# The last 128 tokens of the gate stage: from features on partitions to tokens on partitions

## The chip, the cores and the metric

The kernel runs on one core of one Trainium2 chip. A core has five engines with a queue each: TensorE (PE in the profile, with its weight loads as PEld), VectorE (DVE), ScalarE (ACT), GpSimd (POOL) and SyncE (SP, which here only issues transfers). Each queue is worked off in order; the queues wait for one another by semaphores. The metric is the time of one execution on the device, in microseconds (us).

## The reference

One encoder layer over 1024 tokens of 1024 features, in float32. Only its end matters here:

```python
hn = rmsnorm(h, norm_ple_g)
gate = jax.nn.sigmoid(hn @ w_ple_gate + b_ple_gate)   # (1024 x 1024) @ (1024 x 1024)
h = h + gate * (p @ w_ple)                            # p: 1024 x 256
return rmsnorm(h, final_g)                            # y = x * rsqrt(mean(x*x) + eps) * g
```

Before it come a pooling mixer and a chunked attention with their projections, and a gated MLP.

## The kernel before

All activations lie transposed in SBUF: features on the 128 partitions in eight tiles (`H[0]` to `H[7]`), tokens along the free axis. Every large product is done as three matmuls (`mm3`, L130 to L132) on operands that are split into a high and a low part (`hi`, `lo`), in a reduced-precision float32 format; the three add up in one PSUM bank. Moving operands are at most 512 columns wide.

The gate stage (from `ple_mm` on) is the last one. It runs over 18 items `(d, a, b)`: feature tile `d` of the output, tokens `a` to `b`. For the first token half there are eight items of 512 tokens. For the second half there are six items of 512 tokens, and for the last two feature tiles four items of 256 tokens. An item is

- `gate_mm`: 8 x 3 matmuls with the gate weights as stationary operand and the normed activations (`hp[0]` or `hp[1]`) as moving operand, into bank 2, 3 or 7;
- `ple_mm`: 2 x 3 matmuls for the per-layer embedding, into bank 5 or 6;
- `gate_out`: sigmoid on ACT (L1150), times the embedding product on DVE (L1151), added to `H` on DVE (L1152);
- `Norm.add`: square on ACT (L647), added up over feature tiles on DVE (L649);
- a scaling of the item by the final norm's gain on ACT (L1205).

With features on partitions, the sum of squares of a token runs over partitions and over feature tiles. So the final norm of a stretch of tokens (a `Norm` object in `lasts`) ends in four more steps: `sums`, one small matmul against a column of ones for each 128 tokens (L655, L657) with a VectorE step (L658) and a power of -1/2 on POOL (L659); `rows`, which spreads the result over all partitions by PE transposes (L663); and `emit`, which multiplies `H` by it on DVE (L1169) in pieces of 1024 elements per partition and issues a 512 KB store for each piece (L1170), by turns on the SP and the ACT queue. The second half has two such norms, for tokens 512 to 767 and 768 to 1023. The first of these is emitted in the middle of the last item; the second stands alone at the end of the kernel.

PE's order is the order of the code. Of the other engines a scheduler sets the order, except where `keep_in_program_order` pins it.

Of the kernel before, what the change touches and what calls it, by code (L numbers as in the profile page):

```python
# [6 lines left out]
F32 = mybir.dt.float32  # L7
F32R = mybir.dt.float32r
AF = mybir.ActivationFunctionType
ALU = mybir.AluOpType  # L10

P = 128
SEQ = 1024
D = 1024
KT = D // P
# [7 lines left out]
MAX_REL = 128  # L23
WINDOWS = (2, 4, 8, 16)
HIST = 16
EPS = 1e-6
BIG = 3.0e38

# [53 lines left out]


def trunk(tc, xT, pT, vecs, w_qk0, w_in, w_v, bias, counts, pool_w, w_out, w_up, w_down,
          w_gate, w_ple, out):
    nc = tc.nc
    act, dve, pe, pool, sp = nc.scalar, nc.vector, nc.tensor, nc.gpsimd, nc.sync

    with tc.tile_pool(name="sb", bufs=1) as sb, \
# [6 lines left out]
        def region(z, dt):  # L96
            a, b = spans[z]
            return sb.tile([P, (b - a) * 256], dt, name=f"R{z}", tag=f"R{z}")

        Rs = [region(z, F32R) for z in range(5)]  # L100
        F = sb.tile([P, 15616], F32, name="F")
        ident = sb.tile([P, P], F32, name="ident")
        vec = sb.tile([P, NVEC], F32, name="vec")
        small = sb.tile([P, 80], F32, name="small")
        PS = pp.tile([P, 8, 512], F32, name="PS")
# [16 lines left out]
        def f(kb, n):  # L122
            return F[:, int(kb * KW):int(kb * KW) + n]
# [15 lines left out]
        mhalf = small[:, 0:1]  # L139
# [27 lines left out]
        qk32 = [f(38 + 4 * s, 1024) for s in range(2)]  # L167
        U = f(38, 4 * (HIST + SEQ)).rearrange("p (g t) -> p g t", g=4)
        T1 = f(54.25, 272)
# [75 lines left out]
        for t in range(NTOK):  # L245
            pe.matmul(PS[:, 7, t:t + 1], xraw[0][:, t * P:(t + 1) * P], ones, start=True, stop=True)
        dve.tensor_scalar(rstd_tok, PS[:, 7, 0:NTOK], 1.0 / D, EPS, ALU.mult, ALU.add)
        pool.tensor_tensor(rstd_tok, rstd_tok, mhalf.to_broadcast([P, NTOK]), ALU.pow)
# [79 lines left out]
        def keys(i):  # L328
            t = i % NTOK
            k0 = max(0, t - 4)  # L330
            return i // NTOK, t, k0, t + 1 - k0
# [111 lines left out]
        def project_u(g):  # L443
            def evac(h, ps):
                hs = slice(h * 512, (h + 1) * 512)
                dve.tensor_tensor(U[:, g, HIST + h * 512:HIST + (h + 1) * 512], ps, rstd_bc[:, hs], ALU.mult)
            pool.memset(U[:, g, 0:HIST], 0.0)
            yield from project(g, evac)
            win = WINDOWS[g]
            eng = pool if g >= 2 else dve  # L450
            for q in (3, 2, 1, 0):
                n = HIST + 256
                u = U[:, g, q * 256:q * 256 + n]
# [9 lines left out]
        def pool_out(g, q, u, src, eng):  # L463

            win, n, f0 = WINDOWS[g], HIST + 256, HIST
            if q == 0:
                f0 = HIST + win
                eng.tensor_tensor(src[:, HIST:f0], src[:, HIST:f0], cnt[:, 0:win], ALU.mult)
# [103 lines left out]
        for i in range(NI + 3):  # L572
            if i >= 7:
                sums_due(i, (i - 6) // 2)
            if i < NI:
                h, t, k0, nk = keys(i)
# [43 lines left out]
        H = [f(8 + 4 * d, 1024) for d in range(KT)]  # L620
# [6 lines left out]
        class Norm:  # L627
# [24 lines left out]
            def sums(self):  # L652
                for t in range(self.nt):
                    ts_ = slice(t * P, (t + 1) * P)
                    pe.matmul(self.ssq[:, t:t + 1], self.acc[:, ts_], ones, start=True, stop=self.whole)  # L655
                    if not self.whole:
                        pe.matmul(self.ssq[:, t:t + 1], self.q[:, ts_], ones, start=False, stop=True)  # L657
                dve.tensor_scalar(self.s, self.ssq, 1.0 / D, EPS, ALU.mult, ALU.add)  # L658
                pool.tensor_tensor(self.s, self.s, mhalf.to_broadcast([P, self.nt]), ALU.pow)  # L659
# [149 lines left out]
        for z, d in enumerate((0, 4, 1, 5, 2, 6, 3, 7)):  # L809
            k = z // 2  # L810
# [218 lines left out]
        wg = [None] * KT  # L1029
        hp = [None, None]  # L1030
# [90 lines left out]
        pt = [(r(8 * k, 1024), r(8 * k + 4, 1024)) for k in range(2)]  # L1121
        wp = [(r(16 + 8 * k, 1024), r(20 + 8 * k, 1024)) for k in range(2)]
# [11 lines left out]
        def gate_mm(d, a, b, bank, middle=None):  # L1134
            ds_ = slice(d * P, (d + 1) * P)
            ts_ = slice(a % 512, a % 512 + b - a)
            for k in range(KT):
                hi, lo = hp[a // 512][k]
                mm3(PS[:, bank, 0:b - a], wg[k][:, ds_], wg[k][:, 1024:2048][:, ds_], hi[:, ts_], lo[:, ts_],
                    k == 0, k == KT - 1)  # L1140
                if k == 3 and middle:
                    middle()
# [21 lines left out]
        def emit(norm):  # L1164

            n = 1024 // (norm.nt * P)
            for z, d in enumerate(range(0, KT, n)):
                h_ = HH[:, d:d + n, norm.ts]
                dve.tensor_tensor(h_, h_, norm.out.unsqueeze(1).to_broadcast([P, n, norm.nt * P]), ALU.mult)  # L1169
                (sp, act)[z % 2].dma_start(  # L1170
                    out[d * P:(d + n) * P, norm.ts].rearrange("(e p) t -> p e t", p=P), h_)

        zt = [f(2 * s, 512) for s in range(4)]
        acc, sq = f(52.25, 512), f(54.25, 512)
        lasts = {(0, 512): Norm(slice(0, 512), f(40, 512), [f(42, 512)], 4, 1),
                 (512, 1024): Norm(slice(512, 1024), acc, [sq], 4, 1)}
        for z, ab in enumerate(((512, 768), (768, 1024))):
            zs = slice(256 * z, 256 * z + 256)
            lasts[ab] = Norm(slice(*ab), acc[:, zs], [sq[:, zs]], 4, z, z == 0)
            lasts[ab].n = 6  # L1180
        ple_banks, gate_banks = (5, 6), (2, 3, 7)
        items = ([(d, 0, 512) for d in range(KT)] + [(d, 512, 1024) for d in range(6)]
                 + [(d, a, a + 256) for a in (512, 768) for d in (6, 7)])

        def ended(ab):
            lasts[ab].rows()
            emit(lasts[ab])

        for i, (d, a, b) in enumerate(items):
            gate_mm(d, a, b, gate_banks[i % 3], (lambda: ended((512, 768))) if i == 17 else None)  # L1190
            if i == 0:
                continue
            if i == 16:
                lasts[512, 768].sums()
            if i == 1:
                norm_b.sums()
            if i == 2:
                norm_b.rows(rst2[:, HS[1]])
            for z in ((0, 1) if i == 1 else (i,)):
                dz, az, bz = items[z]  # L1200
                ple_mm(dz, az, bz, ple_banks[z % 2])
                gate_out(dz, az, bz, gate_banks[z % 3], ple_banks[z % 2], zt[z % 4])
                lasts[az, bz].add(dz)
                hz = H[dz][:, az:bz]
                act.activation(hz, hz, AF.Copy, scale=vec[:, C_GL + dz:C_GL + dz + 1])  # L1205
            if 3 <= i <= 6:
                normed2(2 * i - 6)
                normed2(2 * i - 5)
            if i == 8:
                lasts[0, 512].sums()  # L1210
            if i == 9:
                ended((0, 512))
        lasts[768, 1024].sums()
        ended((768, 1024))
        b_pool.__exit__(None, None, None)


def _layout(i):

    c = np.ascontiguousarray  # L1220
    x = i["x"][0]
    w_in = i["w_in"][0]
    w_up = i["w_up"][0]
    d = {}
    d["xT"] = c(x.T).reshape(KT, P, SEQ)
    d["pT"] = c(i["p"][0, 0].T).reshape(2, P, SEQ)

    def cols(v, n):
        return np.asarray(v).reshape(n, P).T

    cw = i["conv_w"][0]
    d["vecs"] = c(np.concatenate(
        [cols(i["norm_mix_g"][0], KT)] + [cols(cw[j], NF) for j in range(3)]
        + [cols(i["conv_b"][0], NF), cols(i["pool_b"][0], 4), cols(i["pool_scale"][0], 4)]
        + [cols(i[n], KT) for n in ("norm_ffn_g", "norm_ple_g", "b_ple_gate", "final_g")], axis=1))
    wt = w_in.reshape(KT, P, 16, P).transpose(2, 1, 0, 3)
    d["w_qk0"] = c(np.concatenate([wt[4], wt[8]], axis=2)).reshape(P, KT * 2 * P)
    d["w_in"] = c(wt[:12]).reshape(12, P, D)
    d["w_v"] = c(w_in[:, 1536:].reshape(KT, P, 2, 256).transpose(2, 1, 0, 3)).reshape(2, P, KT * 256)
    ii = np.arange(P)[:, None] + 512 - np.arange(BANDT * P)[None, :]  # L1240
    d["bias"] = c(i["rel_bias"][0][:, np.clip(ii, -MAX_REL, MAX_REL) + MAX_REL])
    d["counts"] = np.tile((1.0 / np.arange(1, 17)).astype(np.float32)[None, :], (P, 1))
    d["pool_w"] = c(i["pool_w"][0].transpose(1, 0, 2)).reshape(P, 512)
    d["w_out"] = c(i["w_out"][0].reshape(8, P, 2, 512).transpose(2, 0, 1, 3))
    d["w_up"] = c(w_up.reshape(KT, P, 2, NF, P).transpose(3, 2, 1, 0, 4)).reshape(NF, 2, P, D)
    d["w_down"] = c(i["w_down"][0].reshape(NF, P, D))
    d["w_gate"] = c(i["w_ple_gate"][0].reshape(KT, P, D))
    d["w_ple"] = c(i["w_ple"][0].reshape(2, P, D))
    return d


# [15 lines left out]
```

## Time and profile before

| | us |
|---|---|
| median of 3 runs | 1146.85 (1145.53 to 1147.0) |
| the profiled execution, its own time | 1144.99 |
| its span, first to last instruction | 1143.2 |
| busy PE / DVE / ACT / POOL in the span | 1124.7 / 886.8 / 580.4 / 282.3 |
| granted TensorE clock, mean | 0.996 |

The profiled execution is 1.86 us (0.16%) below the median of the other runs; 1.79 us of its time lie outside the span. Times below are us from the start of the span. In rows of the timeline the first number is the start, the second the duration; "x2" means two instructions that are drawn as one, from the first's start to the last's end. The matmul durations hold the pipeline's latency, so that two neighbours overlap: the pace is read from the starts.

### The profile page before, as it was taken

How to read it: one execution, taken by the hardware profiler on the slowest of the kernel's cores; microseconds unless marked ns; L12 is line 12 of the kernel's file. 1: busy time of each engine (PE TensorE's matmuls, PEld its weight loads, DVE VectorE, ACT ScalarE, POOL GpSimd, SP SyncE). 2: the span in 40 equal slices, each digit the busy share in tenths (PEclk: the TensorE clock that was granted, in tenths of full speed). 3: DMA queues.
4: the chain of work that ended last, by engine and by line, in shares of the span. 5: the costliest groups of instructions: out<-in, count | busy, mean ns of one | idle time of the engine just before them, and what ended most of it. 6: DMA issues, size and time to landing. Idle time of an engine off the chain costs nothing.

```text
span 1143.2 us, 15272 instructions
## 1 busy us (share of the span) xinstructions
PE 1124.7 (98%) x5517; PEld 944.7 (83%) x5517; DVE 886.8 (78%) x1371; ACT 580.4 (51%) x1001; POOL 282.3 (25%) x307
## 2 busy tenths in 40 slices
PE   9999999999999999999999999999999999999996
PEld 7988998888888877878888888888888888888886
DVE  7678878779656788888889888889797789757344
ACT  8568677765555543434443434344444567545222
POOL 0013334275002234645453434232000000000000
PEclk9999999999999999999999999999999999999998
DMA  7134756533500376554444321112683555310012
GB/s 265 38 86 114 164 118 178 121 85 130 184 19 10 137 213 175 137 138 123 149 118 112 91 100 39 65 38 78 222 281 109 167 185 169 115 48 1 1 74 75
DMA packets 62572, 133.46 MB, mean 117 GB/s; under 512 B 7392, under 2 KB 9696, under 8 KB 62048
## 3 DMA queue, kind: packets, MB, share of 16 engines
q1 hardware_dynamic: 49552, 100.96, 26.5%
q0 software_dynamic: 11200, 29.37, 12.8%
q10 hardware_dynamic: 1744, 2.17, 0.5%
q8 instruction: 43, 0.70, 0.3%
q14 instruction: 33, 0.27, 0.1%
HBM read 116.73 MB, written 45.09 MB: 142 GB/s over the span
## 4 chain that ended last, share of the span: by engine, by line
PE 83%; DVE 6%; ACT 3%; issue 3%; DMA 3%; POOL 1%; SPq 0%; DVEq 0%; POOLq 0%; ACTq 0%
PE PS L130 26%; PE PS L131 26%; PE PS L132 26%; PE PS L370 2%; ACT F L356 1%; PE PS L387 1%; PE PS L388 1%; DVE R L136 1%; DMA X<-in_w_up 1%; DVE B L378 1%; POOL SD L556 1%; DVE F L346 1%; DMA F<-in_xT 1%; DMA GD<-F 1%; POOL X L759 1%
## 5 line engine op out<-in xcount | busy, mean ns | idle before, releaser
L130 PE MATMUL PS<-R,R 128*128 128x512 f32 (+1 forms) x932 | 359.6, 386 | 0.6 <-ACT R L230 0.6
L132 PE MATMUL PS<-R,R 128*128 128x512 f32 (+1 forms) x932 | 355.8, 382 | 0.9 <-DVE R L136 0.9
L131 PE MATMUL PS<-R,R 128*128 128x512 f32 x868 | 338.0, 389 | 0.5 <-DVE R L231 0.5
L132 PEld LDWEIGHTS PS<-R,R 128*128 128x128 f32 x932 | 175.3, 188 | 35.6 <-DVE R L136 1.3
L130 PEld LDWEIGHTS PS<-R,R 128*128 128x128 f32 x932 | 175.3, 188 | 33.0 <-ACT R L230 1.0
L131 PEld LDWEIGHTS PS<-R,R 128*128 128x128 f32 x868 | 163.3, 188 | 32.7 <-DVE R L231 1.4
L131 PE MATMUL PS<-B 128*128 128x512 f32 x316 | 123.1, 390 | 0.4 <-DVE B L136 0.4
L130 PE MATMUL PS<-B 128*128 128x512 f32 x316 | 123.2, 390 | 0.0
L132 PE MATMUL PS<-B 128*128 128x512 f32 x316 | 123.1, 389 | 0.0
L759 POOL TENSOR_TENSOR X<-X 128x512 f32<-128x512 f32 x46 | 84.7, 1841 | 141.3 <-DMA X<-in_w_up 69.9
L135 ACT ACTIVATE R<-X 128x512 fp32r<-128x512 f32 x102 | 64.3, 632 | 103.5 <-PE PS L131 58.3
L135 ACT ACTIVATE R<-F 128x512 fp32r<-128x512 f32 (+1 forms) x116 | 69.2, 613 | 71.0 <-PE PS L131 35.7
L135 ACT ACTIVATE B<-F 128x512 fp32r<-128x512 f32 (+1 forms) x94 | 61.0, 649 | 82.8 <-PE PS L131 55.7
L136 DVE TENSOR_TENSOR R<-X,R 128x512 fp32r<-128x512 f32 x102 | 102.5, 1005 | 0.0
L136 DVE TENSOR_TENSOR R<-F,R 128x512 fp32r<-128x512 f32 (+1 forms) x112 | 85.7, 777 | 20.2 <-ACT R L135 19.6
L659 POOL TENSOR_TENSOR small<-small 128x4 f32<-128x4 f32 (+1 forms) x7 | 8.1, 1159 | 335.9 <-DVE small L658 335.9
L136 DVE TENSOR_TENSOR B<-F,B 128x512 fp32r<-128x512 f32 (+1 forms) x94 | 66.8, 714 | 29.1 <-ACT B L135 28.8
L131 PEld LDWEIGHTS PS<-B 128*128 128x128 f32 x316 | 59.3, 188 | 13.0 <-DVE B L136 0.8
L130 PEld LDWEIGHTS PS<-B 128*128 128x128 f32 x316 | 59.3, 188 | 12.4
L132 PEld LDWEIGHTS PS<-B 128*128 128x128 f32 x316 | 59.3, 188 | 12.4
L131 PE MATMUL PS<-B,R 128*128 128x256 f32 (+1 forms) x208 | 64.0, 308 | 0.0
L356 ACT ACTIVATE F<-F,small 128x640 f32<-128x640 f32 (+2 forms) x64 | 44.5, 696 | 24.3 <-DVE small L354 16.9
(171 smaller groups left out, 2081.8 us busy)
## 6 DMA issues: line engine op xcount, KB each, us to landing
SD<-in_w_down POOLq DMA_DIRECT2D x66, 256.0 KB, 4.9
X<-in_w_up SPq DMA_DIRECT2D x56, 256.0 KB, 3.0
F<-SD SPq DMA_DIRECT2D x49, 256.0 KB, 2.7
GD<-F SPq DMA_DIRECT2D x22, 512.0 KB, 2.6
R<-GD SPq DMA_DIRECT2D x44, 256.0 KB, 5.4
F<-in_w_down SPq DMA_DIRECT2D x33, 256.0 KB, 3.2
F<-in_w_up SPq DMA_DIRECT2D x29, 256.0 KB, 2.9
SD<-SD POOLq DMA_DIRECT2D x28, 256.0 KB, 3.1
```

The costliest lines, as they stand in the source:

```text
L130: pe.matmul(ps, ahi, bhi, start=first, stop=False, skip_group_check=more)
L131: pe.matmul(ps, ahi, blo, start=False, stop=False, skip_group_check=more)
L132: pe.matmul(ps, alo, bhi, start=False, stop=last, skip_group_check=more)
L135: act.activation(hi, src, AF.Copy)
L136: dve.tensor_tensor(lo, src, rv(hi), ALU.subtract)
L346: dve.tensor_tensor_reduce(S.rearrange("p (a b) -> p a b", a=2), PS[:, 4:6, 0:320], b.rearrange("p (a b) -> p a b", a=2), 1.0, BIG, ALU.ad ...
L356: act.activation(S[:, 0:n], S[:, 0:n], AF.Exp, bias=s_[:, 0:1], scale=-1.0, accum_out=s_[:, 1:2])
L370: pe.transpose(pst[:, j * P:(j + 1) * P], S[:, j * P:(j + 1) * P], ident)
L378: dve.tensor_tensor(lo, pst, rv(hi), ALU.subtract)
L387: pe.matmul(O, V[:, k, h], pt[:, 0, idx], start=n_ == 0, stop=False)
L388: pe.matmul(O, V[:, k, h], pt[:, 1, idx], start=False, stop=n_ == len(ks) - 1)
L759: pool.tensor_tensor(rawu[to], rawu[a], rawu[b], op)
```

## The change

The second token half is cut in two. Tokens 512 to 895 (`BODY` is 896) are computed as before, but as eight items of 384 tokens instead of six of 512 and four of 256, with one norm for all 384. The last 128 tokens (`TAIL`) are computed with tokens on partitions:

- eight PE transposes turn `H` of these tokens into `h_t` (banks 0 and 1);
- `ple_tail` and `gate_tail` swap the two operands of the products: the activations become the stationary operand, the weights the moving one, in slices of 512, 256 and 256 features;
- the arithmetic of a slice is a pinned sequence of six instructions: bias added (DVE), sigmoid (ACT), times the embedding product (DVE), plus `h_t` (DVE), square with a sum along the row (ACT, into `ss`), times the final gain (DVE);
- bias and gain now vary along the free axis, so a new input `rows` (128 x 2048, 1 MB, each row the same) is loaded on the SP queue into the region that held `hp[0]`;
- the norm's sum is along the row, so it needs no small matmuls and no transposes: two small DVE steps, one POOL power on 128x1, and then one scaling by that column, half of the features on ACT with a 256 KB store on the ACT queue, half on DVE with a 256 KB store on the SP queue;
- the norm of tokens 512 to 895 has its `sums` and `rows` between the matmuls of the first slice of the tail; its four stores all go by SP.

The output is one flat array, the first 896 tokens by features and the last 128 by tokens, put together outside of the timed part.

```diff
         def emit(norm):
             n = 1024 // (norm.nt * P)
+            dst = out[0:BODY * D].rearrange("(d t) -> d t", t=BODY)
             for z, d in enumerate(range(0, KT, n)):
                 h_ = HH[:, d:d + n, norm.ts]
                 dve.tensor_tensor(h_, h_, norm.out.unsqueeze(1).to_broadcast([P, n, norm.nt * P]), ALU.mult)
-                (sp, act)[z % 2].dma_start(
-                    out[d * P:(d + n) * P, norm.ts].rearrange("(e p) t -> p e t", p=P), h_)
+                (sp, act)[z % 2 if norm.ts.start == 0 else 0].dma_start(
+                    dst[d * P:(d + n) * P, norm.ts].rearrange("(e p) t -> p e t", p=P), h_)
...
-                 (512, 1024): Norm(slice(512, 1024), acc, [sq], 4, 1)}
-        for z, ab in enumerate(((512, 768), (768, 1024))):
...
+                 (512, BODY): Norm(slice(512, BODY), f(52.25, 512 - TAIL), [f(54.25, 512 - TAIL)], 4, 2)}
...
-        items = ([(d, 0, 512) for d in range(KT)] + [(d, 512, 1024) for d in range(6)]
-                 + [(d, a, a + 256) for a in (512, 768) for d in (6, 7)])
+        items = [(d, a, b) for a, b in ((0, 512), (512, BODY)) for d in range(KT)]
...
-            gate_mm(d, a, b, gate_banks[i % 3], (lambda: ended((512, 768))) if i == 17 else None)
+            gate_mm(d, a, b, gate_banks[i % 3])
...
-            if i == 16:
-                lasts[512, 768].sums()
...
-        lasts[768, 1024].sums()
-        ended((768, 1024))
+        Rs[2] = region(2, F32)
+        row_b, row_g, x_t, xg, o_t = [r(32 + 4 * k, D) for k in range(5)]
+        sp.dma_start(r(32, 2 * D), rows)
...
+        def ple_tail(z):
+            zs = slice(z * 512, (z + 1) * 512)
+            for k in range(2):
+                mm3(ple_t[:, zs], pt[k][0][:, BODY:SEQ], pt[k][1][:, BODY:SEQ], wp[k][0][:, zs], wp[k][1][:, zs],
+                    k == 0, k == 1)
+
+        def gate_tail(z, a, b, ps, hooks=()):
+            for k in range(KT):
+                hi, lo = [t[:, BODY - 512:512] for t in hp[1][k]]
+                mm3(ps, hi, lo, wg[k][:, a:b], wg[k][:, 1024 + a:1024 + b], k == 0, k == KT - 1)
+                if k in dict(hooks):
+                    dict(hooks)[k]()
+            t = x_t[:, a:b]
+            for ins in (lambda: dve.tensor_tensor(t, ps, row_b[:, a:b], ALU.add),
+                        lambda: act.activation(t, t, AF.Sigmoid),
+                        lambda: dve.tensor_tensor(t, ple_t[:, a:b], t, ALU.mult),
+                        lambda: dve.tensor_tensor(t, h_t[:, a:b], t, ALU.add),
+                        lambda: act.activation(o_t[:, a:b], t, AF.Square, accum_out=ss[:, z:z + 1]),
+                        lambda: dve.tensor_tensor(xg[:, a:b], t, row_g[:, a:b], ALU.mult)):
+                tc.keep_in_program_order(ins())
+
+        for d in range(KT):
+            pe.transpose(h_t[:, d * P:(d + 1) * P], H[d][:, BODY:SEQ], ident)
+        ple_tail(0)
+        gate_tail(0, 0, 512, PS[:, 3], ((3, lasts[512, BODY].sums), (6, lambda: ended((512, BODY)))))
+        ple_tail(1)
+        gate_tail(1, 512, 768, PS[:, 7, 0:256])
+        dve.tensor_scalar(ss[:, 3:4], ss[:, 0:1], ss[:, 1:2], D * EPS, ALU.add, ALU.add)
+        gate_tail(2, 768, 1024, PS[:, 7, 256:512])
+        s = ss[:, 4:5]
+        dve.tensor_scalar(s, ss[:, 2:3], ss[:, 3:4], 1.0 / D, ALU.add, ALU.mult)
+        pool.tensor_tensor(s, s, mhalf, ALU.pow)
+        dst = out[BODY * D:].rearrange("(t d) -> t d", d=D)
+        act.activation(o_t[:, 0:512], xg[:, 0:512], AF.Copy, scale=s)
+        act.dma_start(dst[:, 0:512], o_t[:, 0:512])
+        dve.tensor_scalar(o_t[:, 512:D], xg[:, 512:D], s, None, ALU.mult)
+        sp.dma_start(dst[:, 512:D], o_t[:, 512:D])
```

Lines of the changed kernel stand two or three further down than before (L660 is the old L658, L1172 the old L1169, L1173 the old L1170). Ahead of the second half's items no engine's order changes.

DVE's queue at the end of the program before, from the first sums step of the second half on: in a row of the queue stand the line, the operation, the output and the inputs (F is the SBUF buffer that holds `H`, PS is PSUM, small holds the norms' columns), and the shape.

```order
L658 TENSOR_SCALAR small<-PS 128x2
L1151 TENSOR_TENSOR F<-PS,F 128x256
L1152 TENSOR_TENSOR F<-F 128x256
L649 TENSOR_TENSOR F<-F 128x256
L1169 TENSOR_TENSOR F<-F,PS 128x4x256 x2
```

The two scalings of the first 256 tokens stand there ahead of the last item's L1151 and L1152; then come the last L658 and the last two scalings, L1169.

The same queue in the changed kernel, again from the sums step on (R_8392 is the region with the new rows and the tail's buffers):

```order
L660 TENSOR_SCALAR small<-PS 128x3
L1172 TENSOR_TENSOR F<-F,PS 128x2x384 x4
L1230 TENSOR_TENSOR R_8392<-PS,R_8392 128x512
L1232 TENSOR_TENSOR R_8392<-PS,R_8392 128x512
L1233 TENSOR_TENSOR R_8392<-PS,R_8392 128x512
L1235 TENSOR_TENSOR R_8392<-R_8392 128x512
L1230 TENSOR_TENSOR R_8392<-PS,R_8392 128x256
L1232 TENSOR_TENSOR R_8392<-PS,R_8392 128x256
L1233 TENSOR_TENSOR R_8392<-PS,R_8392 128x256
L1235 TENSOR_TENSOR R_8392<-R_8392 128x256
L1244 TENSOR_SCALAR small<-small 128x1
```

All four scalings of the body (L1172) have moved ahead of the whole arithmetic of the tail, and the three slices of the tail follow one another; the third slice's four instructions, L1247 and L1252 come last.

SP's queue at the end of the program before (its last loads are those of the embedding, then the stores):

```order
L929 DMA F<-in_w_down 128x512 x12
L929 DMA F<-in_pT 128x512 x2
L929 DMA F<-in_w_ple 128x512 x4
L1170 DMA out_h<-F 128x2x512 x2
L1170 DMA out_h<-F 128x4x256 x2
```

And in the changed kernel:

```order
L931 DMA F<-in_w_ple 128x512 x4
L931 DMA F<-in_pT 128x512 x2
L1212 DMA R_8392<-in_rows 128x2048
L1173 DMA out_h<-F 128x2x512 x2
L1173 DMA out_h<-F 128x2x384 x4
L1253 DMA out_h<-R_8392 128x512
```

The load of the new rows stands ahead of all stores, and the store of half of the tail behind the four of the body.

More of the change, by code (lines that the diff above doesn't have):

```diff
@@ L25 @@
 HIST = 16
+TAIL = 128
+BODY = SEQ - TAIL
 EPS = 1e-6
@@ L84, in trunk @@
 def trunk(tc, xT, pT, vecs, w_qk0, w_in, w_v, bias, counts, pool_w, w_out, w_up, w_down,
-          w_gate, w_ple, out):
+          w_gate, w_ple, rows, out):
     nc = tc.nc
@@ L1169, in emit @@
                 dve.tensor_tensor(h_, h_, norm.out.unsqueeze(1).to_broadcast([P, n, norm.nt * P]), ALU.mult)
-                (sp, act)[z % 2].dma_start(
-                    out[d * P:(d + n) * P, norm.ts].rearrange("(e p) t -> p e t", p=P), h_)
+                (sp, act)[z % 2 if norm.ts.start == 0 else 0].dma_start(
+                    dst[d * P:(d + n) * P, norm.ts].rearrange("(e p) t -> p e t", p=P), h_)
         zt = [f(2 * s, 512) for s in range(4)]
-        acc, sq = f(52.25, 512), f(54.25, 512)
         lasts = {(0, 512): Norm(slice(0, 512), f(40, 512), [f(42, 512)], 4, 1),
-                 (512, 1024): Norm(slice(512, 1024), acc, [sq], 4, 1)}
-        for z, ab in enumerate(((512, 768), (768, 1024))):
-            zs = slice(256 * z, 256 * z + 256)
-            lasts[ab] = Norm(slice(*ab), acc[:, zs], [sq[:, zs]], 4, z, z == 0)
-            lasts[ab].n = 6
+                 (512, BODY): Norm(slice(512, BODY), f(52.25, 512 - TAIL), [f(54.25, 512 - TAIL)], 4, 2)}
         ple_banks, gate_banks = (5, 6), (2, 3, 7)
-        items = ([(d, 0, 512) for d in range(KT)] + [(d, 512, 1024) for d in range(6)]
-                 + [(d, a, a + 256) for a in (512, 768) for d in (6, 7)])
+        items = [(d, a, b) for a, b in ((0, 512), (512, BODY)) for d in range(KT)]
         def ended(ab):
@@ L1212, in trunk @@
                 ended((0, 512))
-        lasts[768, 1024].sums()
-        ended((768, 1024))
+        Rs[2] = region(2, F32)
+        row_b, row_g, x_t, xg, o_t = [r(32 + 4 * k, D) for k in range(5)]
+        sp.dma_start(r(32, 2 * D), rows)
+        ss = small[:, 40:45]
+        wide = PS.rearrange("p a b -> p (a b)")
+        h_t, ple_t = wide[:, 0:D], wide[:, 5 * 512:5 * 512 + D]
+        def ple_tail(z):
[3 more added lines that the diff above has]
+                    k == 0, k == 1)
@@ L1248, in _layout @@
     d["w_ple"] = c(i["w_ple"][0].reshape(2, P, D))
+    d["rows"] = np.tile(np.concatenate([i["b_ple_gate"][0], i["final_g"]])[None, :], (P, 1))
     return d
@@ L1261 @@
         args.append(nc.dram_tensor(f"in_{name}", a.shape, mybir.dt.from_np(a.dtype), kind="ExternalInput").ap())
-    out = nc.dram_tensor("out_h", (D, SEQ), F32, kind="ExternalOutput").ap()
+    out = nc.dram_tensor("out_h", (D * SEQ,), F32, kind="ExternalOutput").ap()
     with tile.TileContext(nc) as tc:
@@ L1265 @@
     r = run_bass_kernel_spmd(nc, [arrays], core_ids=[0])
-    return np.ascontiguousarray(r.results[0]["out_h"].T).reshape(1, SEQ, D)
+    o = r.results[0]["out_h"]
+    body = o[:BODY * D].reshape(D, BODY).T
+    return np.ascontiguousarray(np.concatenate([body, o[BODY * D:].reshape(TAIL, D)])).reshape(1, SEQ, D)
```

## The prediction

> **What bounds the kernel now.** I read the page's first part, then the busy time by stretches at the end, the chain that ended last, and the timeline of the gate stage.
>
> ```profile
> span 1143.2 us, 15272 instructions
> PE 1124.7 (98%) x5517; PEld 944.7 (83%) x5517; DVE 886.8 (78%) x1371; ACT 580.4 (51%) x1001; POOL 282.3 (25%) x307
> 1136.00:1144.00 8.00, 0.00 (x0) 0.00 (x0) 2.35 (x2) 0.00 (x0) 0.00 (x0) 0.50 0.39 132
> ```
>
> PE works almost without a gap, so matmul work can only be moved, not hidden. The exception is the end: in the last 8 us PE does nothing. What ends last there is the chain of the second norm of 256 tokens:
>
> ```profile
> 1134.48 0.74 POOLq L1263
> 1135.27 0.70 PE PS L663 x2
> 1136.00 1.22 DVE F L1169
> 1137.22 1.13 DVEq L1263
> ```
>
> Power on POOL, two transposes on a PE that has cooled to half its clock, two scalings on DVE, then the stores. The change replaces this end. So two questions count: when PE ends its last matmul, and how long the path from there to the end of the last store is.
>
> **PE up to the tail.** The timeline of PE gives the paces:
>
> ```profile
> 1073.26 0.40 PE L130 MATMUL PS<-B,R 128*128 128x512 f32 x1
> 1080.26 0.95 PE L655 MATMUL PS<-small,F 128*128 128x1 f32 x8
> 1116.54 0.28 PE L130 MATMUL PS<-B,R 128*128 128x256 f32 x1
> 1126.60 0.50 PE L655 MATMUL PS<-small,F 128*128 128x1 f32 x4
> 1126.96 0.36 PE L130 MATMUL PS<-R,R 128*128 128x256 f32 x1
> 1129.20 0.38 PE L663 MATMUL PS<-ident,small 128*128 128x128 f32 x2
> 1129.34 0.36 PE L130 MATMUL PS<-B,R 128*128 128x256 f32 x1
> 1131.45 0.28 PE L132 MATMUL PS<-R,R 128*128 128x256 f32 x1
> ...
> 136.56 0.34 PE L352 MATMUL PS<-R 128*128 128x384 f32 x1
> 136.74 0.33 PE L353 MATMUL PS<-R 128*128 128x384 f32 x1
> 136.91 0.28 PE L130 MATMUL PS<-R,R 128*128 128x256 f32 x1
> ```
>
> One item of 512 tokens is 30 matmuls: 1073.26 to 1080.26, 0.2333 us each. Between the first 256-wide one (1116.54) and the sums (1126.60) lie 84: 0.1198 each. The only 384-wide ones of the kernel, in the attention, are 0.175 each (136.56 to 136.91, two). Half way between the neighbours would be 0.1767, and 512-wide ones between 0.2267 and 0.2333 would scale to 0.17 to 0.18; I take the row, 0.175, and keep 0.172 to 0.18.
>
> Before, six items of 512 take 180 x 0.2333 = 42.0 from 1073.26, and with 1.28 for the first half's sums and transposes among them the split items begin at 1116.54. After, eight items of 384 take 240 x 0.175 = 42.0. The sums and transposes of the first half stay. So the tail begins at the same 1116.54 (bounds -0.7, +1.2).
>
> **PE in the tail.** Before, from 1116.54 to 1131.57, 15.0 us. After, piece by piece:
>
> ```profile
> 201.94 0.76 PE L370 MATMUL PS<-ident,F 128*128 128x128 f32 x5
> 202.47 0.48 PE L130 MATMUL PS<-R,B 128*128 128x512 f32 x1
> ...
> L370 PE MATMUL PS<-ident,F 128*128 128x128 f32 x240 | 37.3, 275 | 1.6 <-DVE B L378 1.1
> ```
>
> - Eight transposes of `H`: the attention's take 0.53 for five, 0.106 each, plus 0.08 that the next matmul loses (0.48 long instead of 0.40): 0.93.
> - First embedding slice: 6 x 0.2333 = 1.40.
> - First gate slice: 24 x 0.2333 = 5.60, plus three sums and three transposes. Two tokens' columns of sums cost 0.36 + 0.08 (1126.60 to 1126.96, and the next matmul's longer start), so three 0.67; two transposes cost 0.14 + 0.08, three 0.30.
> - Second embedding slice 1.40; two gate slices of 256, 48 x 0.12 = 5.76.
>
> Together 16.06: PE ends at 1132.60, 1.0 us later than before, with the last result about 0.16 behind the pace, at 1132.76. The transposes are the addition, the rest evens out. The `rows` wait for POOL: the sums end near 1122.4, POOL needs at most the 1.34 of its mean for four columns, so it is done by 1124.1, and PE comes to the `rows` at 1116.54 + 0.93 + 1.40 + 2.80 + 0.67 + 2.10 = 1124.44. No stall, with 0.3 us to spare.
>
> The trace speaks against counting the transposes at their own length: in the group's row each lasts 275 ns, but five start within 0.53 us. The Trainium skill ("TensorE: Matmul & The Clock Gate", part on the PE-mode transpose) gives about 275 ns for a 128x128 transpose in a kernel and warns that its latency dominates; counted so, one behind the other, eight would cost 2.2 and the end would come 1.3 later. The trace agrees with its length but not with a pace of that size, so the sum goes by the starts.
>
> **DVE and ACT in the tail.** This is where I see the new bound. The durations:
>
> ```profile
> 1117.53 0.69 DVE L1152 TENSOR_TENSOR F<-F 128x512 f32<-128x512 f32 x1
> 1118.26 0.63 ACT L647 ACTIVATE F<-F 128x512 f32<-128x512 f32 x1 [2.22 <-DVE F L1152]
> 1118.92 0.73 ACT L1205 ACTIVATE F<-F,vec 128x512 f32<-128x512 f32 x1
> 1123.99 0.42 DVE L1151 TENSOR_TENSOR F<-PS,F 128x256 f32<-128x256 f32 x1 [1.79 <-PE PS L132]
> 1124.45 0.42 DVE L1152 TENSOR_TENSOR F<-F 128x256 f32<-128x256 f32 x1
> 1124.91 0.42 ACT L647 ACTIVATE F<-F 128x256 f32<-128x256 f32 x1 [1.22 <-DVE F L1152]
> 1129.74 2.35 DVE L1169 TENSOR_TENSOR F<-F,PS 128x1024 f32<-128x1024 f32 x2
> 1134.28 0.16 DVE L658 TENSOR_SCALAR small<-PS 128x2 f32<-128x2 f32 x1 [1.40 <-PE PS L657]
> 1134.52 0.70 POOL L659 TENSOR_TENSOR small<-small 128x2 f32<-128x2 f32 x1 [6.44 <-DVE small L658]
> L356 ACT ACTIVATION_READ_ACCUMULATOR F<-F,small 128x1 f32 x64 | 12.0, 188 | 0.0
> L566 POOL COPY small<-F 64x1 f32<-64x1 f32 x27 | 7.3, 271 | 97.0 <-DVE F L394 91.6 <-issue 5.2
> L361 DVE TENSOR_SCALAR F<-F,small 128x512 f32<-128x512 f32 x5 | 2.4, 484 | 0.1
> ```
>
> A dependent step starts 0.04 after the one it waits for (1123.99 + 0.42 to 1124.45, and from there to ACT at 1124.91); an independent one on DVE 0.09 before the end of its forerunner (2.35 for two of 1.22).
>
> The transposed norm is ready at 1124.44 + 0.49 + 0.04 = 1125.0. In DVE's queue the four scalings of 768 elements now come first; the 1024-element ones go at 1.13 each, so 0.87 each. The tail's arithmetic starts at 1125.0 + 3.46 = 1128.46, though its first product is complete at 1125.6. Slice 1 (512 wide): DVE 0.69, ACT sigmoid 0.63, DVE 0.69, DVE 0.69, and the next L1235 0.69; with four hops of 0.04 and 0.09 of overlap the second slice's first step starts at 1131.92. Slice 2 (256 wide): 0.42 four times with hops, then ACT's square 0.42 with 0.19 to read its sum (the attention's sums show that read as an instruction of 188 ns): the square ends at 1134.36, L1244 waits for it, ends at 1134.56, and slice 3 starts at 1134.48, overlapping. Its product has been there since 1132.76. So DVE, not PE, sets the last slice, by 1.7 us.
>
> Slice 3: 0.42 + 0.42 + 0.42 + 0.42 with four hops, square 0.42 + 0.19, hop: L1247 at 1136.96, 0.16; POOL, 0.08 on, at 1137.20. A power of one column is not in the trace: four take 1.34 as above, two 0.70, which leaves 0.35 for one; the nearest single-column step on POOL, a copy, takes 0.27. I take 0.37, bounds 0.27 and 0.70. Then from 1137.61 DVE scales 512 features in 0.48 and ACT 512 in 0.73 (L1205, which also takes its factor from a column): the stores are issued at 1138.13 on SP and 1138.37 on ACT.
>
> If ACT's sigmoid costs as much as L1205 for its width rather than L647 (its bias may be read from a column), it is 0.1 longer three times: +0.3 at most.
>
> **The stores.**
>
> ```profile
> 1137.24 0.37 SPq L1170 DMA_DIRECT2D out_h<-F  x1
> 1138.38 0.38 ACTq L1170 DMA_DIRECT2D out_h<-F  x1
> 1138.00:1139.00 1.00, 0.00 (x0) 0.00 (x0) 0.35 (x1) 0.00 (x0) 0.00 (x0) 0.50 0.85 286
> 1141.00:1142.00 1.00, 0.00 (x0) 0.00 (x0) 0.00 (x0) 0.00 (x0) 0.00 (x0) 0.50 0.23 74
> ```
>
> The last two stores of 512 KB keep the DMA engines busy from 1138.15 to 1141.23 (0.85 and 0.23 of these slices), 0.91 after the SP issue, at 340 GB/s; the span ends 2.0 later. After, two of 256 KB: from 1138.13 + 0.91 = 1139.04, half the bytes in 1.54, to 1140.58. With the same 2.0 behind it the span ends at 1142.55. If the new row-wise stores (2 KB pieces instead of 1 KB) gained nothing, it would end at 1143.2 again. The four body stores, 1.5 MB issued from 1126 on, need some 4.7 us at that rate and are through by 1132.
>
> The 1 MB load of `rows`:
>
> ```profile
> 1090.30 47.32 SPq L1170 DMA_DIRECT2D out_h<-F  x4
> ```
>
> SP issues its first store at 1090.30, and the load stands ahead of it and waits only for the last matmul of the first half (about 1072.8). It has 55 us until the tail's first addition and passes nothing that is late: cost nothing.
>
> **Sum.** PE +1.0 (to 1132.60 from 1131.57); from there to the last issue 5.8 instead of 6.8, so the last issue is where it was, 1138.37 against 1138.38; stores -0.65. Net -0.65 us against the span of 1143.2. The profiled execution lies 1.86 under the median shown; I subtract from the median: 1146.85 - 0.65 = 1146.2. A run-to-run spread of about 0.2% is all that a measurement here can tell from no change, that is 2.3 us.
>
> **Rivals.**
> - *DVE is not behind.* If the scalings and slices ran ahead of the pinned order or faster, slice 3 would start at PE's 1132.76: 1.7 earlier, 1144.5, just faster by 0.2%. The order of DVE's queue speaks against it; DVE would have to save 1.7 of the 9.5 us from 1125.0 on.
> - *384-wide matmuls are cheaper than 0.175.* From 256 to 512 columns the pace grows by 0.1135, so by 0.0568 for 128; a matmul that cost its columns alone would take 0.170 at 384, and 240 x 0.005 = 1.2 more would go: 1145.0. To be faster by 0.2% it must be 0.168 or less (1.65 / 240 below 0.175), against the one row of its kind. The Trainium skill ("TensorE: Matmul & The Clock Gate", back-to-back issue gap) gives N / 2.4 + 2.5 ns for warm matmuls; for 384 that is 162.5 ns, an estimate by which 3.0 would go and 1143.2 come out. The trace's 119.8 ns for 256 and 233.3 for 512 lie 11 and 18 above that law, so it is not what I use.
> - *384-wide matmuls are dearer.* A weight load shows 188 ns:
>
> ```profile
> L132 PEld LDWEIGHTS PS<-R,R 128*128 128x128 f32 x932 | 175.3, 188 | 35.6 <-DVE R L136 1.3
> ```
>
>   If it set the pace, 240 x 0.013 = 3.1: 1149.3, slower. It decides above 0.187. The 256-wide stream at 0.1198 with the same loads speaks against it.
> - *The tail's chain of some 25 hops is longer than summed*: 0.1 more at each is 2.5, 1148.7, slower from 0.12 on. The trace's hops in this same stage are 0.03 to 0.08.
>
> **How the numbers follow.** My sum 0.78; DVE not behind 0.08; cheaper matmuls 0.05; dearer matmuls 0.03; longer chain 0.06. The first holds no change of 0.2% (within 1144.55 and 1149.1) over its bounds: -0.7 to +1.2 for the pace, -0.1 to +0.3 for POOL, +0.3 for ACT, +0.65 for the stores, and 0.7 for where a median of few runs falls. Faster 0.14, same 0.77, slower 0.09. Range 1144.5 to 1148.3.
>
> **What would show it.** After: 384-wide starts 0.175 apart; the transposes of `H` near 1116.6; the first L1230 starting when the last L1172 ends, some 3 us behind its last matmul; the last L1230 about 1.7 after PE's end; last issues near 1138.4; the DMA engines busy for 1.5 us at the end. The prediction is wrong if PE waits at `rows`, if the last L1230 waits for PE, or if the pace is off by more than 0.01.

## The result, and the profile after

The changed kernel takes 1148.18 us (median of 22 runs) against 1146.52 for the kernel before on the same chips: ratio 1.0018, 95% interval 1.0009 to 1.0026, so some 2.1 us slower (the medians alone differ by 1.66). One of the 22 runs took 2328.16 us; it is left out of the ratio. The forecast was 1146.2, 0.65 faster than before, in a range of 1144.5 to 1148.3: the range holds the time, but the sign is wrong.

The profiled execution of the changed kernel is one of its longest: 1151.29 us, with a span 6.3 us longer than before. Its page:

```profile
span 1149.5 us, 15343 instructions
PE 1128.8 (98%) x5542; PEld 953.6 (83%) x5542; DVE 891.2 (78%) x1380; ACT 578.0 (50%) x1005; POOL 281.3 (24%) x307
```

The stages ahead of the change run the same instructions in both kernels, so I count from the first matmul of the second token half, which the change begins with. It stands at 1073.26 before and here at 1077.35, in the first row of the timeline below. Most of the 6.3 us, 4.1, thus arises ahead of the change; a further profile of the same kernel (the last of the runs below) will show that this part is chance. From that first matmul to the end of the span it is 1143.2 - 1073.26 = 69.94 us before and 1149.5 - 1077.35 = 72.15 after: 2.2 us more, about the measured loss. This time is called the stretch below.

The timeline of PE, DVE, POOL and ACT after it, with the wait in brackets (idle time, and what ended it):

```profile
1077.35 0.34 PE L132 MATMUL PS<-B,R 128*128 128x384 f32 x1
1121.06 1.04 PE L1239 MATMUL PS<-ident,F 128*128 128x128 f32 x8
1128.90 0.49 PE L665 MATMUL PS<-ident,small 128*128 128x128 f32 x3
1129.43 3.55 DVE L1172 TENSOR_TENSOR F<-F,PS 128x768 f32<-128x768 f32 x4 [2.38 <-PE PS L665]
1132.89 0.68 DVE L1230 TENSOR_TENSOR R<-PS,R 128x512 f32<-128x512 f32 x1
1134.01 0.28 PE L134 MATMUL PS<-R,B 128*128 128x256 f32 x1
1136.34 0.42 DVE L1230 TENSOR_TENSOR R<-PS,R 128x256 f32<-128x256 f32 x1
1136.81 0.39 PE L132 MATMUL PS<-R,B 128*128 128x256 f32 x1 [2.52 <-DVE R L1230]
1137.98 0.31 PE L132 MATMUL PS<-R,B 128*128 128x256 f32 x1
1138.52 0.41 PE L132 MATMUL PS<-R,B 128*128 128x256 f32 x1
1140.86 0.41 PE L134 MATMUL PS<-R,B 128*128 128x256 f32 x1
1141.31 0.42 DVE L1230 TENSOR_TENSOR R<-PS,R 128x256 f32<-128x256 f32 x1 [2.40 <-PE PS L134]
1143.97 0.55 POOL L1248 TENSOR_TENSOR small<-small 128x1 f32<-128x1 f32 x1 [15.99 <-DVE small L1247]
1145.31 0.35 ACTq L1251 DMA_DIRECT2D out_h<-R  x1
```

PE ends the second slice of the tail at 1134.01 + 0.28 and then stands still for 2.52 us, until DVE has read that slice's product (the second L1230, 1136.34). Only then does the third slice begin. Its first nine matmuls go at 0.12 us; from 1138 on they take 0.21. The busy time by stretches says why (the column before the last two is the granted clock of PE):

```profile
1137.00:1138.00 1.00, 1.00 (x10) 1.00 (x10) 0.73 (x2) 0.21 (x1) 0.00 (x0) 1.00 0.00 0
1138.00:1139.00 1.00, 1.00 (x8) 1.00 (x7) 0.76 (x3) 0.51 (x2) 0.00 (x0) 0.55 0.00 0
1139.00:1140.00 1.00, 1.00 (x6) 1.00 (x6) 0.00 (x0) 0.00 (x0) 0.00 (x0) 0.50 0.00 0
```

The clock fell to half about 1.3 us after PE had resumed (in the second profile of this kernel, at the end of the runs below, it fell at another point). And now DVE, which since the four scalings had not waited for PE, waits 2.40 us for the third slice's product: a wait of PE for DVE and one of DVE for PE, one after the other, on the path that sets the end.

The reason lies in two lines of the change: `gate_tail(1, ..., PS[:, 7, 0:256])` and `gate_tail(2, ..., PS[:, 7, 256:512])`. The second and the third slice share PSUM bank 7. They touch different columns, but the wait goes by the bank: PE starts to write it only when DVE has read the other product out of it, and with the third slice in another bank the wait is gone (the first run below). The Trainium skill ("PSUM — Partial Sum Buffer", on bank collisions) says that two engines must not use one bank at once on the same partitions, whatever the address, and that the hardware itself does not stall, so that software must put a dependency there. The trace agrees as far as it can: the wait is there, with 2.52 us. What the hardware would do without it no run here shows.

All steps against the forecast, in us from the first matmul of the second half (the forecast's times less 1073.26, the measured ones less 1077.35):

| step | forecast | measured | difference |
|---|---|---|---|
| transposes of `H` begin | 43.28 | 43.71 | +0.43 |
| `rows` of the body's norm on PE | 51.18 | 51.55 | +0.37 |
| first L1172 on DVE | 51.74 | 52.08 | +0.34 |
| addition of slice 1 | 55.20 | 55.54 | +0.34 |
| addition of slice 2 | 58.66 | 58.99 | +0.33 |
| addition of slice 3 | 61.22 | 63.96 | +2.74 |
| last issue, on ACT | 65.11 | 67.96 | +2.85 |
| end of the span | 69.29 | 72.15 | +2.86 |

The leap of 2.4 us at slice 3 is the whole change of sign: without it the stretch would still be some 0.2 shorter than before.

### The profile page after: what moved, and what is told of

It is laid out like the page before. It is cut to its first block, busy times and chain, and to the rows that moved or that the text cites. A ratio compares the mean times of both kernels' runs of the same rounds, so it can differ in the third digit from the quotient of the medians.

```text
span 1149.5 us, 15343 instructions
## 1 busy us (share of the span) xinstructions
PE 1128.8 (98%) x5542; PEld 953.6 (83%) x5542; DVE 891.2 (78%) x1380; ACT 578.0 (50%) x1005; POOL 281.3 (24%) x307
## 3 DMA queue, kind: packets, MB, share of 16 engines
q10 hardware_dynamic: 832, 1.38, 0.3%
## 4 chain that ended last, share of the span: by engine, by line
PE 81%; DVE 8%; issue 4%; DMA 3%; ACT 2%; POOL 1%; SPq 0%; POOLq 0%; DVEq 0%; ACTq 0%
PE PS L132 25%; PE PS L133 25%; PE PS L134 25%; DVE R L138 2%; PE PS L372 2%; PE PS L389 1%; PE PS L390 1%; DVE V L867 1%; DVE B L380 1%; ACT F L358 1%; DMA GD<-F 1%; DMA F<-in_xT 1%; DMA F<-in_w_down 1%; DMA X<-in_w_up 1%; DVE F L888 1%
## 5 line engine op out<-in xcount | busy, mean ns | idle before, releaser
L132 PE MATMUL PS<-R,R 128*128 128x512 f32 (+2 forms) x932 | 360.6, 387 | 2.0 <-ACT R L137 1.0
L134 PE MATMUL PS<-R,R 128*128 128x512 f32 (+2 forms) x932 | 357.2, 383 | 2.1 <-DVE R L138 2.1
L133 PE MATMUL PS<-R,R 128*128 128x512 f32 (+1 forms) x868 | 338.7, 390 | 0.5 <-DVE R L233 0.5
L133 PE MATMUL PS<-B,R 128*128 128x256 f32 (+1 forms) x192 | 57.7, 301 | 0.0
```

The costliest lines, as they stand in the source:

```text
L132: pe.matmul(ps, ahi, bhi, start=first, stop=False, skip_group_check=more)
L133: pe.matmul(ps, ahi, blo, start=False, stop=False, skip_group_check=more)
L134: pe.matmul(ps, alo, bhi, start=False, stop=last, skip_group_check=more)
```

## The experiments

**The third slice in a bank of its own.** Theory A is the account above; theory B puts the loss elsewhere.

```diff
-        gate_tail(2, 768, 1024, PS[:, 7, 256:512])
+        gate_tail(2, 768, 1024, PS[:, 4, 0:256])
```

> The third slice's product of the tail goes to bank 4 instead of the second half of bank 7; nothing else changes. Counted from the first matmul of the second token half to the end of the span, before takes 69.94 us and the changed kernel 72.15. Theory A (PE waits 2.5 us at the third slice because DVE still has to read the second slice out of the same bank, and then runs half of that slice at half clock): the idle time of PE before the third slice is gone, its 24 matmuls keep 0.12 us, the third L1230 starts straight behind L1244 at about 61.6 instead of 63.96 from that first matmul, the end comes at about 69.8, ratio to before 1.000. Theory B (the loss lies in the pace of the 384-wide items and the transposes, and the wait at the third slice is covered by DVE being late anyway): the end stays near 72, ratio 1.002.

Measured: 1146.02 us against 1147.19 for before on the chip of this and the next three runs, ratio to before 0.9994 (0.9978 to 1.0009). The interval touches that of the changed kernel (1.0009 to 1.0026), so the gain is read from the profile. The timeline, with the first matmul of the second half, the last of the third slice, DVE's third addition and the last issue:

```profile
1075.69 0.34 PE L132 MATMUL PS<-B,R 128*128 128x384 f32 x1
1135.16 0.28 PE L134 MATMUL PS<-R,B 128*128 128x256 f32 x1
1137.16 0.41 DVE L1230 TENSOR_TENSOR R<-PS,R 128x256 f32<-128x256 f32 x1
1141.15 0.35 ACTq L1251 DMA_DIRECT2D out_h<-R  x1
```

The span is 1145.3 us, so the stretch is 69.61, against 72.15: one bank number is worth 2.5 us, all of the 2.2 that were lost and a little more. PE no longer waits in the tail. The third addition starts 61.47 after the first matmul, close to the 61.22 of the forecast, and its product has lain there since 59.75 (1135.16 + 0.28). So the picture of DVE as the bound of the tail was right, once PE is let go. Theory B is out.

**The clock's share.** The wait stays, but PE is given work in it.

```diff
+        for _ in range(10):
+            pe.matmul(PS[:, 4], hp[1][0][0][:, 0:P], wg[0][:, 0:512], start=True, stop=True)
         gate_tail(2, 768, 1024, PS[:, 7, 256:512])
```

> The shared bank 7 and so the wait stay; ten 512-wide matmuls into the otherwise idle bank 4, whose result nobody reads, stand between the second and the third slice, 2.3 us of PE work inside the 2.5 us that PE waits. Theory A1 (the slow half of the third slice, 0.21 us a matmul, is the clock that the idle time halved): the granted clock stays 1.00, all 24 matmuls go at 0.12, the third L1230 starts 1.4 us earlier, end at about 70.7 from the first matmul of the second half, ratio to before 1.0007. Theory A2 (the slow pace comes from the bank that PE and DVE share): the pace of 0.21 stays and so does the end, 72.1, ratio 1.002.

Measured: 1147.12 us, ratio 1.0004 (0.9988 to 1.002); the times alone don't tell it from the changed kernel or from the one before. The profile does:

```profile
1073.70 0.34 PE L132 MATMUL PS<-B,R 128*128 128x384 f32 x1
1133.15 0.39 PE L132 MATMUL PS<-R,B 128*128 128x256 f32 x1 [0.19 <-DVE R L1230]
1135.98 0.28 PE L134 MATMUL PS<-R,B 128*128 128x256 f32 x1
1136.30 0.42 DVE L1230 TENSOR_TENSOR R<-PS,R 128x256 f32<-128x256 f32 x1 [1.04 <-PE PS L134]
1135.00:1136.00 1.00, 1.00 (x11) 1.00 (x9) 0.21 (x1) 0.01 (x1) 0.00 (x0) 1.00 0.00 0
```

PE still starts the third slice only when DVE has read the second, but it has been idle for 0.19 us, the clock stays at 1.00, and the slice goes at full pace. The third addition comes 1136.30 - 1073.70 = 62.60 after the first matmul, 1.36 earlier than with the idle wait; the span is 1144.5 and the stretch 70.80. So of the 2.5 us about 1.35 were the halved clock, and some 1.1 the wait itself (62.60 against 61.47 with a bank of its own), beyond the time by which DVE was late anyway. That PE and DVE share a bank is not what slows the matmuls (A2): the bank is still shared here.

**The scalings between the steps.** The bank stays shared. Of the body's four scalings on DVE, the first stays ahead of the tail's arithmetic; one moves into the wait for the sigmoid in each of the first two slices, and one between these slices, each with its store.

```diff
+        def scale_body(z):
+            h_ = HH[:, 2 * z:2 * z + 2, body.ts]
+            tc.keep_in_program_order(dve.tensor_tensor(
+                h_, h_, body.out.unsqueeze(1).to_broadcast([P, 2, body.nt * P]), ALU.mult))
...
-        gate_tail(0, 0, 512, PS[:, 3], ((3, lasts[512, BODY].sums), (6, lambda: ended((512, BODY)))))
+        gate_tail(0, 0, 512, PS[:, 3], ((3, body.sums), (6, body.rows)), (("ahead", 0), (1, 1), (5, 2)))
...
-        gate_tail(1, 512, 768, PS[:, 7, 0:256])
+        gate_tail(1, 512, 768, PS[:, 7, 0:256], (), ((1, 3),))
```

(A pair `(n, z)` of the last argument puts scaling `z` behind step `n` of the slice's six, counted from 0; `"ahead"` puts it ahead of them.)

> The four scalings of the body (tokens 512 to 895) are pinned between the steps of the tail's first two slices on DVE instead of ahead of them; the shared bank 7 stays. Theory A with the scalings as its origin: the first L1230 step starts about 2.6 us earlier, the second slice's product is read about 1.7 us earlier, PE idles some 0.9 us instead of 2.5 at the third slice and the clock stays 1.00; the third slice's addition starts at about 61 from the first matmul of the second half, end at 69.1, ratio to before 0.9993. Theory B (DVE's order does not matter, the body's pace does): 72, ratio 1.002.

Measured: 1145.39 us, ratio 0.9989 (0.9974 to 1.0004), span 1141.7:

```profile
1072.64 0.34 PE L132 MATMUL PS<-B,R 128*128 128x384 f32 x1
1130.44 0.38 PE L132 MATMUL PS<-R,B 128*128 128x256 f32 x1 [0.86 <-DVE R L1242]
1133.56 0.42 DVE L1242 TENSOR_TENSOR R<-PS,R 128x256 f32<-128x256 f32 x1 [0.72 <-PE PS L134]
1137.56 0.35 ACTq L1265 DMA_DIRECT2D out_h<-R  x1
```

(L1242 is the addition, L1230 in the changed kernel.) PE waits 0.86 us instead of 2.52, for the same bank, and keeps its clock. The stretch is 69.06. So the wait was as long as it was because the scalings stood ahead of the tail in DVE's queue: the bank made PE dependent on DVE, and DVE's order made it late.

**Both together.** The edit is the sum of the two.

> Own bank for the third slice and the scalings between the steps. Theory A: PE never waits, the third slice's addition starts when its product is there, about 60.2 from the first matmul of the second half, end at 68.4, ratio to before 0.9987, faster than before. Theory B: 72, ratio 1.002. A third theory (the tail is bound by the stores, not by DVE): no gain over the run with the own bank alone, 69.8, ratio 1.000.

Measured: 1145.81 us, ratio 0.9982 (0.9968 to 0.9995), span 1145.2:

```profile
1076.86 0.34 PE L132 MATMUL PS<-B,R 128*128 128x384 f32 x1
1136.33 0.28 PE L134 MATMUL PS<-R,B 128*128 128x256 f32 x1
1136.96 0.41 DVE L1242 TENSOR_TENSOR R<-PS,R 128x256 f32<-128x256 f32 x1
```

The stretch is 68.34, 3.8 less than with the change as it was made and 1.6 less than before. It is the first version whose ratio lies below 1 with its whole interval; the medians alone differ by less than the ratio says (1.38 us, or 0.12%), so the size is taken from the stretch. The stores do not bind: the gain came through to the end. The third addition, 60.10 from the first matmul, still starts 0.35 us after its product is complete (1136.33 + 0.28, that is 59.75).

**The side steps of slice 2 later.** On DVE two instructions stood between: the second slice's gain product, and the sum over two slices, which waits for ACT's square.

```diff
...
+                if n_ == 5 and z == 1:
+                    held.append(ins)
+                    continue
                 tc.keep_in_program_order(ins())
+                if n_ == 1 and z == 2:
+                    tc.keep_in_program_order(held.pop()())
+                if n_ == 4 and z == 2:
+                    tc.keep_in_program_order(
+                        dve.tensor_scalar(ss[:, 3:4], ss[:, 0:1], ss[:, 1:2], D * EPS, ALU.add, ALU.add))
...
-        dve.tensor_scalar(ss[:, 3:4], ss[:, 0:1], ss[:, 1:2], D * EPS, ALU.add, ALU.add)
```

> As the run with both remedies, and on DVE the second slice's gain product and the sum over the first two slices (which waits for ACT's square) no longer stand ahead of the third slice's addition but in its waits for ACT. There the third addition starts 60.1 from the first matmul of the second half, while its product is complete about 59.4. Theory A (DVE's order still costs 0.6 us there): the addition starts at about 59.45, the end comes at 67.7 instead of 68.34, ratio to before about 0.998. Rival (the stores or the small steps bind): 68.3 as before it.

Measured: 1143.47 us against 1146.63 for before on this chip, ratio 0.9978 (0.9964 to 0.9993), span 1141.6:

```profile
1073.63 0.34 PE L132 MATMUL PS<-B,R 128*128 128x384 f32 x1
1133.10 0.28 PE L134 MATMUL PS<-R,B 128*128 128x256 f32 x1
1133.41 0.42 DVE L1243 TENSOR_TENSOR R<-PS,R 128x256 f32<-128x256 f32 x1 [0.39 <-PE PS L134]
1137.41 0.35 ACTq L1274 DMA_DIRECT2D out_h<-R  x1
```

Now DVE waits for PE, 0.39 us. The addition comes at 59.78, right behind its product, which is complete at 59.75, as it was in the run above; the 59.4 of the expectation was too early, so that 0.35 us and not 0.6 were to be gained. The stretch is 67.97, 0.37 less than in the run above and 2.0 us less than before, somewhat less than the ratio says (2.5) but inside its interval. The intervals of this run and the one above overlap, so that it is the faster of the two is read from the profiles (67.97 against 68.34), not from the times. It beats both kernels.

**The changed kernel once more**, on the chip of the run above.

> The changed kernel itself, on the chip of the other run. If the loss is the wait at the third slice and what follows it, the stretch from the first matmul of the second half to the end is 72.1 again and PE waits 2.5 us there again, whatever the time ahead of the gate stage is; ratio to before 1.002. If the 4 us by which its first profile was later ahead of the gate stage belong to the change, that point lies near 1077 again; if they are chance, anywhere between 1072 and 1077.

Measured: 1147.4 us, ratio 1.0011 (0.9994 to 1.0028), span 1144.9:

```profile
1072.74 0.34 PE L132 MATMUL PS<-B,R 128*128 128x384 f32 x1
1132.19 0.58 PE L132 MATMUL PS<-R,B 128*128 128x256 f32 x1 [2.52 <-DVE R L1230]
1135.48 0.28 PE L132 MATMUL PS<-R,B 128*128 128x256 f32 x1
1136.74 0.42 DVE L1230 TENSOR_TENSOR R<-PS,R 128x256 f32<-128x256 f32 x1 [2.45 <-PE PS L134]
PE PS L132 <- DVE R L1230: 2.5, 1, 2.5
```

The first matmul of the second half stands at 1072.74 this time, 4.6 us earlier than in the first profile and 0.5 earlier than before: that part was chance. The stretch from there is 72.16 against 72.15, with the same wait of 2.5. The clock, though, fell at another point: here it was already at half when PE resumed at 1132.19, and it was back in full at 1135.48, for the last nine matmuls. In both profiles 3.2 us of the third slice went at half clock, its end in the first and its beginning in the second. It is the profile's stretch, not the whole time, that repeats to a few hundredths; the interval of these twelve runs by itself holds no change, and it is the 22 runs above that show the loss.

## Why the prediction was wrong

- **The step that failed** is in "PE in the tail" and "DVE and ACT in the tail": "PE ends at 1132.60", with one wait looked at, that for the `rows`, and for slice 3 "Its product has been there since 1132.76. So DVE, not PE, sets the last slice". The sum let PE run on by itself while DVE fell behind. It did not ask whose PSUM bank the third slice writes. With DVE late at slice 2, which the sum itself had put at 1131.92, PE could not begin slice 3 there at 1129.7 as its own sum had it, but only after that step, some 2.5 us later. Every number for this stood in the sum; the bank that ties them was in the code of the change, and the wait is one of PE's own. The runs: own bank 69.61, shared 72.15. An estimate from the prediction's own terms: with slice 3 beginning on PE at 1132.38 (1131.92 + 0.42 + 0.04) and 24 matmuls of 0.12 behind it, its product is complete at 1135.42 and not at 1132.76, the addition starts 0.94 later, and the gain of 0.65 becomes a loss of 0.3, before any change of the clock.
- **What followed from it** was not foreseen either: with 2.5 us of idle time PE's clock fell to half for 3.2 us of the third slice, 1.35 us more. The chain shown before had a PE "that has cooled to half its clock", and the change was taken to have left that behind.
- **Right, as mechanism and in size**: DVE is behind because the four scalings stand ahead (the additions of slices 1 and 2 came within 0.35 us of the forecast, and by the same 0.35 as the stages ahead of them); the path from the last addition to the last issue, 3.89 forecast and 4.00 measured; the stores, 4.18 from the last issue to the end forecast and 4.19 measured; the load of `rows`, for which no engine waited (it was issued at 1076.2 and took 4.9 us to land). With the bank put right, 69.61 stands against the forecast of 69.29.
- **Mis-sized**: the 384-wide items took 43.71 - 1.28 = 42.43 for 240 matmuls, 0.1768 each instead of 0.175, +0.43 us: half way between the neighbours, 0.1767, which the prediction had named, would have been the better reading here; why, no run shows. POOL's power of one column took 0.55 instead of 0.37, +0.2.
- **Of the rivals** none was the one that came. "DVE is not behind" was refuted as such, and became the gain of the later versions by another order. The cheaper and the dearer 384-wide matmul are out at 0.1768; the longer chain of hops is out with 4.00 us for its second half. "The last L1230 waits for PE" stood among the signs that would make the prediction wrong, and it is the row that did. But no rival had been made of it.
- **The chance of 0.77 for no change of 0.2%** fits a loss of 0.18%; the direction, forecast as a gain of 0.65 us, does not. That the range holds the time is luck: 1148.18 lies just under its upper bound of 1148.3, and none of the terms that the bounds were added up from is the wait that made the loss.

## What to carry to other kernels

When one engine is forecast to fall behind another, look at once for what the faster one will next need back from it: a PSUM bank that two products share is such a thing even if their columns differ, and it turns slack into a wait. The wait of PE here, 2.52 us, cost more than the delay itself, because the clock fell with it; a bank of its own, or ten matmuls without a use in the wait, avoided that. And where the whole time scatters by several us from execution to execution, count from the first instruction that the change touches: the stretch of the changed kernel repeated to 0.01 us in two profiles, and shows what the times alone need dozens of runs for.

## What the runs showed of the hardware

An idle time of 2.52 us came with a halved clock in both profiles of the changed kernel, but the clock fell at different points: in the first 3.8 us after the matmuls had stopped (1.3 after they had resumed), in the second 2.3 us after they had stopped, while PE still waited. Both times it stayed at half for 3.4 us (1138.1 to 1141.5, and 1132.0 to 1135.4). 0.86 us of idle time (scalings between the steps) did nothing. After the last matmul of the tail the clock fell between 1.9 us (side steps of slice 2 later) and 3.9 us (both together) behind it. The Trainium skill ("TensorE: Matmul & The Clock Gate", part 1, on the two states) speaks of an idle window of about 3.4 us, free-running. The changing point and the 3.4 us at half clock fit such a window; but a gap shorter than 3.4 us, with matmuls ahead of it or behind it in the same time, was already enough here. Two profiles can't say whether a wait of 2.52 us always is.

The same shows in the chance part ahead of the gate stage. The busy time by stretches at the start of the MLP, of the first profile of the changed kernel and of the second:

```profile
420.00:440.00 20.00, 18.14 (x68) 14.65 (x68) 16.50 (x23) 7.13 (x12) 5.30 (x7) 0.83 0.77 196
420.00:440.00 20.00, 18.99 (x84) 15.38 (x83) 17.41 (x22) 8.65 (x14) 5.72 (x6) 1.00 0.75 190
```

In the first, PE waited twice within 4 us there (1.03 us from 418.3 on, and 1.86 us up to 421.93), and the mean clock of these 20 us is 0.83; in the second it waited 1.01 us up to 424.08, and the clock kept 1.00. Of the eight profiles of this study, four have a clock below 1.00 there, and three of them have the latest starts of the second half (1075.69 to 1077.35); the fourth starts at 1073.63, among the other four (1072.64 to 1073.70). That the drop causes the late starts was not tried.
